# A second seven-product group in the output projection of a two-layer decoder trunk

## The chip, the core and the metric

The kernel runs on one core of one Trainium2 chip. The metric is the device time of one execution in microseconds (us), from a median of several runs. The engines that matter are TensorE (PE in the profile; PEld is its weight load, which runs beside the matmuls), VectorE (DVE), ScalarE (ACT), GpSimd (POOL, which here only issues DMAs, among them all that add to their destination) and SyncE (SP, which issues the plain loads).

## The reference, cut to what matters

Everything is float32: 256 tokens, 2048 features, 2 layers. In each layer one normalised input is multiplied by a wide matrix `w_in`, three branches (sparse attention, a convolution, stick-breaking attention) are computed from it, gated, projected, merged by sigmoid gates, and put through one output projection. A last norm closes the trunk.

```python
proj = h @ w_in                                   # h = rms_norm(x)
...
y_a = (dsa_attention(...) * silu(za)) @ w_a_out
y_b = (conformer_conv(...) * silu(zb)) @ w_b_out
y_c = (stick_breaking_attention(...) * silu(zc)) @ w_c_out
g = sigmoid(gates).reshape(b, s, N_BRANCH, D_MODEL)
merged = g[:, :, 0] * y_a + g[:, :, 1] * y_b + g[:, :, 2] * y_c
return x + merged @ w_out                         # w_out is 2048 x 2048
```

The change touches the last line, and the order of the work just ahead of it (the last gate columns and the last columns of `y_b`).

## The kernel before, in words

**Units and steps.** A weight matrix is read in units of 256 rows by 512 columns (512 KB, a tile `raw` of 128 x 1024). To keep float32 precision at the speed of the rounded type, each unit is split into two parts: ACT casts `wh` from it (`high`, line 255) and DVE subtracts to get `wl` (`low`, line 259). The activations are split the same way, once. A unit then takes three products: activation high by `wh`, low by `wh`, high by `wl`. A plain step (`plain`, line 431) does this for two token tiles and two 128-row blocks: 12 matmuls of 128x512, eight that need only `wh` and then four that need `wl`.

**Seven products.** `Seven` (line 459) works on the first half of the depth (1024 of 2048 rows) of two neighbouring blocks of 512 columns. Seen as a 2 by 2 block matrix it takes seven block products in place of eight. A product is named M1 to M7 and has two half-steps, a and b: one unit each, used for one token tile alone, so six matmuls. Seven products are 14 half-steps or 84 matmuls; four plain steps for each of two column blocks are 8 units and 96 matmuls. The group pays with sums of weight blocks. `homes` becomes the operand of M5, then of M6, then of M4; `third` that of M7. The sums are made by DVE (`first_sums`, `second_sum`) or by DMAs that POOL issues and that add into the tile (`first_adds` line 501, `last_sum` line 530). Four PSUM banks X, Y, Z, W hold the results; ACT copies X to Y after M1 and W to a buffer after M5, and DVE makes Z (after M6) and W (after M7) by a subtraction (`fork`, line 581). The activation sums that M5, M6, M7 and M3 need (`osums`) are made by `output_sums`.

**The order of the work.** Strings written by hand (`gather`) set the order of the steps: `g.M1a` is the first half of M1 of the group `g`, and a letter alone takes the next plain step of that list. `run` walks the list: the cast and the subtraction of a step are issued two steps (`PARTS`) ahead of its matmuls, its load five more (`LOADS`). Tiles `wh` and `wl` have three buffers each, `raw` has five with a sixth place called `va`. A scheduler then fixes the order on each engine; each engine runs its own list strictly in that order.

**Around the change.** In each layer the last gate group (`h1`, 14 half-steps, with the plain steps `e1` and `f1` of its two column blocks) runs beside the products of `y_b`, 16 plain steps `y1` in four column blocks j = 0 to 3. When a block j is done, DVE merges it (lines 1568, 1569), transposes it in two pieces (line 299), POOL writes it to DRAM (four `z`, line 302) and reads it back (`zy`, line 308), and ACT and DVE split it into the operand `mx` (lines 667, 668), which the output projection needs from depth j*512 on. Then comes the output projection, four column blocks of 512 in lists `qs`. Before the change one group `o` takes two of them for the first half of the depth (blocks 2 and 3 in layer 0, blocks 0 and 1 in the last layer); the other two, `c` and `d`, run in plain steps through all the depth. In the last layer the first half of block 3 is four plain steps into a wide tile, and its second half is a tail of its own that ends the program (lines 1776 on).

Of the kernel before, what the change touches and what calls it, by code (L numbers as in the profile page):

```python
# [51 lines left out]
def trunk(ctx: ExitStack, tc: tile.TileContext, x, w_in, xt, w_a, w_b, w_c, w_out,  # L52
# [63 lines left out]
    class Lazy(list):  # L116
        def __init__(self, n, make):
            super().__init__([None] * n)
            self.make = make
# [21 lines left out]
    def acc_tile():  # L141
        return ap.tile([P, 512], F32, tag="acc", bufs=4, name=nm("acc"))
# [316 lines left out]
    class Seven:  # L459


        def __init__(self, w, cols, act, sums, lead=7, own=None, adds=False, room=None):
            self.banks = banks = {}
            self.steps = {}

            def bank(n):
                if n not in banks:
                    banks[n] = acc_tile()
                return banks[n]
# [33 lines left out]
            def first_sums(h):  # L503
                if own is not None:
                    with in_turn():
                        raw = self.steps["M1", h].raw
                        nc.vector.tensor_add(raw, raw, homes[h])
                    return
                with in_turn():
                    if adds in (1, 2):  # L510
                        nc.vector.tensor_add(homes[h], homes[h], self.steps["M1", h].raw)
                        return
                    nc.vector.tensor_add(third[h], third[h], homes[h])
                    nc.vector.tensor_add(homes[h], homes[h], self.steps["M1", h].raw)

            def second_sum(h):
                if own is not None:
                    if adds:
                        nc.gpsimd.dma_start(homes[h], block(1, 1, h), accum_op=ALU.add)
                    with in_turn():  # L520
                        if not adds:
                            nc.vector.tensor_add(homes[h], homes[h], third[h])
                        nc.vector.tensor_add(third[h], third[h], self.steps["M1", h].raw)
                    return
                with in_turn():
                    nc.vector.tensor_add(homes[h], third[h], self.steps["M1", h].raw)

# [48 lines left out]

            st["M1", 1].at(0, partial(copied, "X", lambda: bank("Y")))
            st["M5", 1].at(0, partial(copied, "W", held))
# [190 lines left out]
    for layer in range(DEPTH):  # L769
# [864 lines left out]
        def merged(b, j, y):  # L1634
            sg = held.pop((b, j), None)
            with in_turn() if b == 1 else nullcontext():
                merge(b, j, y, sg)
            if b == 1:
                with in_turn():
                    turned([mg(j, t) for t in range(NT)], partial(use_m, j), LATER - 3 * (j == 3 and not last), soon=True)  # L1640

        kept_x, acc3 = {}, once(wide_accs)

        def output(q, banks, k0):
            if last and q == 3:
                return [plain(wo, k, q * 512, mx, acc3, k == 0, False) for k in range(0, KC, 2)]

# [66 lines left out]
        zg["M3", 1].at(1, partial(gate_summed, 1))  # L1714
        for i in range(2):
            y1[3][i].at(0, partial(output_sums, i * 2, i * 2 + 1))
        if last:
            zd[3].at(0, lambda: nc.sync.dma_start(fwl[0], fnw.partition_broadcast(P)))
        o = Seven(wo, (p0 * 512, p0 * 512 + 512), mx, osums, 10, None, 3)
        qs = {}  # L1720
        for q in range(4):
            own = q in (p0, p0 + 1)
            banks = (lambda v: lambda: [o.bank(n) for n in v])("ZW" if q - p0 else "XY") if own else None
            qs[q] = output(q, banks, KC if own else 0)
        begin = "g.M1a y g.M5a g.M1b y g.M5b y g.M6a y g.M6b y g.M2a y g.M2b y g.M7a y g.M7b "
# [13 lines left out]
        steps += gather(thin + rest, y=y2[10:], g=g1, c=c1, d=d1)  # L1739
        steps += gather("y*2 " + begin.replace("M6a y", "M6a").replace("M2a y", "M2a") + rest, g=h1, y=y1[:8], c=e1, d=f1)  # L1740
        steps += y1[8:]
        def no_products():
# [9 lines left out]
        steps[at_norm].at(0, norm)  # L1752
        c, d = 2 - p0, 3 - p0
        if last:
            steps += qs[c][:4] + gather(
                "g.M1a d g.M5a g.M1b d g.M5b d g.M6a d g.M6b c g.M2a c g.M2b g.M7a g.M7b g.M3a e g.M3b e g.M4a f g.M4b f c*2 e*2 f*2",
                g=o, c=qs[c][4:], d=qs[d], e=qs[p0], f=qs[p0 + 1])
        else:
            steps += qs[c][:4] + qs[d][:4] + gather(
                "g.M1a c g.M5a g.M1b c g.M5b d g.M6a d g.M6b c g.M2a c g.M2b d g.M7a d g.M7b g.M3a g.M3b e g.M4a e g.M4b e*2 f*4",  # L1760
                g=o, c=qs[c][4:], d=qs[d][4:], e=qs[p0], f=qs[p0 + 1])
        extra = []
# [12 lines left out]
        with tc.high_priority(offset=URGENT):  # L1775
            nc.vector.reduce_sum(known, ssq[:, :, :3], axis=AX.X)
            nc.vector.tensor_scalar(half, known, -0.5 / D, -0.5 * EPS, op0=ALU.mult, op1=ALU.add)
            nc.vector.tensor_scalar(known, known, 1.0 / D, EPS, op0=ALU.mult, op1=ALU.add)

        c0, n = 1536, 512  # L1780
        xc = residual(c0, n)

        head = acc3()
        accs = [head[0], acc_tile()]
# [100 lines left out]
```

## Time and profile before

| | |
|---|---|
| median of 3 runs | 1976.75 us (1975.53 to 1977.73) |
| the profiled execution | 1976.5 us |
| its span, first to last instruction | 1974.6 us |
| granted TensorE clock | 0.998 |
| busy: PE, DVE, ACT, POOL | 1964.4, 1714.8, 1350.3, 248.7 us |
| moved by DMA | 503.67 MB, mean 255 GB/s |

The profile describes one execution. A busy PE is not a PE at its peak, since matmuls overlap and their ends are modelled; the rate is read from the starts in the timeline. Idle time of an engine off the critical chain costs nothing by itself. Around the span lie 1.9 us that the trace does not show.

### The profile page before, as it was taken

The page shows a single profiled execution, that of the slowest core. Times are in us where ns is not written, and L with a number is a line of the kernel's source. Part 1 is how long each engine was busy: PE and PEld are TensorE (multiplying, and loading weights), DVE is VectorE, ACT ScalarE, POOL GpSimd, SP SyncE. Part 2 cuts the span into 40 slices and gives each one's busy share as a digit, 9 for nine tenths or more (in the row PEclk, how much of TensorE's full clock was granted, in tenths as well). Part 3 has the DMA queues.
Part 4 walks back from the last instruction along what each step waited for, and adds up shares of the span by engine and source line. Part 5 has one row for each costly group of instructions (what it writes and reads, how often), then busy time and mean ns, then how long its engine had stood idle before and what let it go on. Part 6 is the DMA issues. An engine that isn't in the chain of part 4 may idle for free.

```text
span 1974.6 us, 26301 instructions
## 1 busy us (share of the span) xinstructions
PE 1964.4 (99%) x9170; PEld 1644.9 (83%) x9170; DVE 1714.8 (87%) x2010; ACT 1350.3 (68%) x1774; POOL 248.7 (13%) x348
## 2 busy tenths in 40 slices
PE   9999999999999999999999999999999999999998
PEld 8888888888888888888888888888888888888886
DVE  8788999988898899878786988999889988898786
ACT  7567657679887667564565666676798876765654
POOL 0011102210200002111100211122101000011010
PEclk9999999999999999999999999999999999999999
DMA  8888769876888889887978887698769898899883
GB/s 277 278 256 271 236 188 313 265 226 190 251 271 262 237 246 298 265 269 274 319 229 277 250 268 234 200 291 279 221 178 283 255 286 245 249 294 270 272 292 136
DMA packets 256261, 503.67 MB, mean 255 GB/s; under 512 B 18496, under 2 KB 31296, under 8 KB 256000
## 3 DMA queue, kind: packets, MB, share of 16 engines
q1 hardware_dynamic: 218560, 408.13, 63.4%
q0 software_dynamic: 35904, 90.72, 18.2%
q10 hardware_dynamic: 1664, 3.15, 0.4%
q8 instruction: 71, 1.16, 0.2%
q14 instruction: 62, 0.51, 0.1%
HBM read 469.16 MB, written 32.77 MB: 254 GB/s over the span
## 4 chain that ended last, share of the span: by engine, by line
PE 99%; DVE 1%; ACT 0%; issue 0%; DVEq 0%
PE acc L270 67%; PE mm L270 28%; PE mm L1269 1%; PE mm L1360 0%; PE mm L1464 0%; PE mm L1411 0%; PE mm L1327 0%; PE mm L1441 0%; PE mm L918 0%; PE mm L1330 0%; PE mm L1240 0%; PE mm L1414 0%; PE mm L1469 0%; DVE wl L259 0%; DVE s L1831 0%; PE mm L1443 0%
## 5 line engine op out<-in xcount | busy, mean ns | idle before, releaser
L270 PE MATMUL acc<-wh,s 128*128 128x512 f32 x3952 | 1006.9, 390 | 0.0
L255 ACT CAST wh<-raw 128x1024 fp32r<-128x1024 f32 (+1 forms) x637 | 664.7, 1046 | 393.4 <-PE acc L270 240.9
L259 DVE TENSOR_TENSOR wl<-raw,wh 128x1024 fp32r<-128x1024 f32 (+1 forms) x638 | 770.0, 1213 | 167.2 <-ACT wh L255 162.8
L270 PEld LDWEIGHTS acc<-wh,s 128*128 128x128 f32 x3952 | 734.8, 188 | 148.2 <-ACT wh L255 0.6
L270 PE MATMUL acc<-wl,s 128*128 128x512 f32 x1784 | 498.9, 390 | 0.1
L270 PEld LDWEIGHTS acc<-wl,s 128*128 128x128 f32 x1784 | 333.8, 188 | 71.5 <-DVE wl L259 2.6
L270 PE MATMUL mm<-wh,s 128*128 128x512 f32 (+1 forms) x1504 | 366.5, 385 | 0.0
L270 PEld LDWEIGHTS mm<-wh,s 128*128 128x128 f32 x1504 | 281.2, 188 | 54.9
L302 POOL DMA_DIRECT2D z<-zt x192 | 114.6, 635 | 682.3 <-DVE zt L299 636.5
L270 PE MATMUL mm<-wl,s 128*128 128x512 f32 (+1 forms) x752 | 198.0, 385 | 0.0
L270 PEld LDWEIGHTS mm<-wl,s 128*128 128x128 f32 x752 | 140.7, 188 | 26.9
L255 ACT CAST wh<-ar 128x1024 fp32r<-128x1024 f32 x92 | 96.9, 1054 | 71.1 <-PE acc L270 32.5
L259 DVE TENSOR_TENSOR wl<-ar,wh 128x1024 fp32r<-128x1024 f32 x92 | 111.8, 1221 | 15.4 <-ACT wh L255 14.4
L259 DVE TENSOR_TENSOR wl<-va,wh 128x1024 fp32r<-128x1024 f32 x53 | 64.7, 1221 | 21.4 <-ACT wh L255 21.2
L255 ACT CAST wh<-va 128x1024 fp32r<-128x1024 f32 x53 | 55.5, 1046 | 32.7 <-PE acc L270 13.9
L308 POOL DMA_DIRECT2D zy<-z x50 | 37.0, 741 | 309.3 <-DVE s L668 86.8
L270 PEld LDWEIGHTS mm<-s,wl 128*128 128x128 f32 x512 | 66.9, 191 | 5.0
L733 DVE SCALAR_TENSOR_TENSOR s<-yT,cst,s 128x256 f32<-128x256 f32 x160 | 69.5, 478 | 0.0
L270 PE MATMUL mm<-s,wl 128*128 128x192 f32 x512 | 66.0, 271 | 0.0
L728 ACT ACTIVATE zt<-yT,cst 128x256 f32<-128x256 f32 x128 | 57.5, 502 | 8.2 <-DVE s L1037 8.0
L728 ACT ACTIVATE ar<-yT,cst 128x256 f32<-128x256 f32 x136 | 60.4, 503 | 2.9 <-PE mm L1330 2.3
L530 POOL DMA_DIRECT2D ar<-in_w_in_dram x28 | 33.8, 1217 | 187.1 <-DVE wl L259 152.0
(293 smaller groups left out, 1581.4 us busy)
## 6 DMA issues: line engine op xcount, KB each, us to landing
raw<-in_w_in_dram SPq DMA_DIRECT2D x496, 512.0 KB, 4.7
raw<-in_w_out_dram SPq DMA_DIRECT2D x50, 512.0 KB, 5.7
zy<-z POOLq DMA_DIRECT2D x48, 512.0 KB, 5.9
z<-zt POOLq DMA_DIRECT2D x184, 128.0 KB, 5.2
ar<-in_w_in_dram SPq DMA_DIRECT2D x28, 512.0 KB, 7.1
ar<-in_w_in_dram POOLq DMA_DIRECT2D x28, 512.0 KB, 8.4
raw<-in_w_a_dram SPq DMA_DIRECT2D x26, 512.0 KB, 6.0
raw<-in_w_b_dram SPq DMA_DIRECT2D x26, 512.0 KB, 5.1
```

The lines of the kernel that those rows point to most:

```text
L255: newest_parts[0] = nc.scalar.copy(u[1], u[0])
L259: newest_parts[1] = sub = nc.vector.tensor_sub(u[2], u[0], u[1].bitcast(F32))
L270: newest[0] = nc.tensor.matmul(o, lhsT, rhs, start=start, stop=stop, skip_group_check=True)
L302: nc.gpsimd.dma_start(z[:, :, :, a, :].rearrange("t b c e -> c (t b) e"), tmp[a * 32:(a + 1) * 32].rearrange("c t b k i -> c (t b) (k i)"))
L308: nc.gpsimd.dma_start(y.rearrange("p (t a) k i -> p t (a k i)", a=4), z.rearrange("t b c a e -> (b c) t (a e)"))
L530: nc.gpsimd.dma_start((homes if own is None else third)[h], block(1, 0, h), accum_op=ALU.add)
L728: nc.scalar.activation(v, yT[:, c, q:q + S], AF.Identity if bias else AF.Copy, scale=wq, **b)
L733: nc.vector.scalar_tensor_tensor(o, yT[:, c, q:q + S], wq, o, op0=ALU.mult, op1=ALU.add)
L1269: nc.tensor.matmul(ps[:, q * S:(q + 1) * S], qi[i][:, hd, :], ki[j][:, 0, :], start=n == 0, stop=n == 2)
```

## The change

A second group `n` is put on the two column blocks that had been plain, so that all four column blocks take the first half of the depth in seven products. Its first products stand earlier: M1 lies among the four plain steps `f1` of the last gate block (in the strings now `h`), M5 and M6 among the last four steps of `y1`, and M2 and M7 follow at once; then the two groups run into one another. The old group `o` gets PSUM from two wide tiles (`wide=True`) in place of four narrow ones, and two of the large slots (`places`) for its `homes` and `third`. Both groups take a new way with their sums (`adds` = 4): `homes` has M1's unit added once, the second sum is `third + homes` and no longer needs M1's raw unit, and what `third` lacked is added by a DMA that POOL issues after that. M1's copy from X to Y comes five steps later in `n` (`copy_at`). The turned block j = 1 is asked for three units sooner, and the activation sums are placed anew.

The diff, without the signature of `Seven` and the removal of the plain steps for the last block:

```diff
                 if n not in banks:
-                    banks[n] = acc_tile()
+                    if wide:
+                        banks.update(zip("XY" if n in "XY" else "ZW", wide_accs()))
+                    else:
+                        banks[n] = acc_tile()
...
-                    if adds in (1, 2):
+                    if adds in (1, 2, 4):
                         nc.vector.tensor_add(homes[h], homes[h], self.steps["M1", h].raw)
                         return
                     nc.vector.tensor_add(third[h], third[h], homes[h])
...
-                    nc.vector.tensor_add(homes[h], third[h], self.steps["M1", h].raw)
+                    nc.vector.tensor_add(homes[h], third[h], homes[h] if adds == 4 else self.steps["M1", h].raw)
+                if adds == 4:
+                    first_adds(h)
...
-            st["M1", 1].at(0, partial(copied, "X", lambda: bank("Y")))
+            st["M1", 1].at(copy_at, partial(copied, "X", lambda: bank("Y")))
...
-                    turned([mg(j, t) for t in range(NT)], partial(use_m, j), LATER - 3 * (j == 3 and not last), soon=True)
+                    turned([mg(j, t) for t in range(NT)], partial(use_m, j), LATER - 3 * (j in (1, 3)), soon=True)
...
-        for i in range(2):
-            y1[3][i].at(0, partial(output_sums, i * 2, i * 2 + 1))
+        for i, st in enumerate((y1[2][3], f1[0])):
+            st.at(0, partial(output_sums, i * 2, i * 2 + 1))
...
-        o = Seven(wo, (p0 * 512, p0 * 512 + 512), mx, osums, 10, None, 3)
...
+        c, d = 2 - p0, 3 - p0
+        places = [once(lambda: slot().rearrange("p a b -> p (a b)")) for _ in range(2)]
+        o = Seven(wo, (p0 * 512, p0 * 512 + 512), mx, osums, 10, None, 4, places, True)
+        n = Seven(wo, (c * 512, d * 512), mx, osums, 9, None, 4, None, False, 5)
...
+        second = "n.M1a h n.M1b h*3 y n.M5a y n.M5b y n.M6a n.M6b y n.M2a n.M2b n.M7a n.M7b "
         if last:
-            steps += qs[c][:4] + gather(
-                "g.M1a d g.M5a g.M1b d g.M5b d g.M6a d g.M6b c g.M2a c g.M2b g.M7a g.M7b g.M3a e g.M3b e g.M4a f g.M4b f c*2 e*2 f*2",
-                g=o, c=qs[c][4:], d=qs[d], e=qs[p0], f=qs[p0 + 1])
+            second += ("o.M1a c o.M1b c o.M5a o.M5b n.M3a n.M3b o.M6a o.M6b n.M4a n.M4b c o.M2a o.M2b o.M7a o.M7b c "
+                       "o.M3a e o.M3b e o.M4a f o.M4b f e*2 f*2")
         else:
...
+            second += ("o.M1a c o.M1b d o.M5a c o.M5b d o.M6a n.M4a o.M6b n.M4b c*2 o.M2a d o.M2b o.M7a o.M7b n.M3a n.M3b d "
+                       "o.M3a e o.M3b e o.M4a e o.M4b e f*4")
```

Counted over the whole program, 24 matmuls of 128x512 fall away (12 in each layer). There are 12 more units to split, in as many casts on ACT and subtractions on DVE, four more DVE sums of 128x1024 (eight for `n`, four fewer for `o`), and four more forks; ACT has four more copies between banks. DMAs of 512 KB: four more on SP, 12 more that add on POOL.

The first place is DVE in the last layer, where the last block of `y1` is merged and `o` begins. Before, in the list of DVE (`wl` are the subtractions of units, `t` and `s` with line 1569 the merge, `zt` the transposes, `ar`, `ph` and `pl` the sums of `o`; the first transposes are those of the block j = 3):

```order
L299 STREAM_TRANSPOSE zt_16533<-s_2546_13909 128x4x4x32 x2
L513 TENSOR_TENSOR ph_16353<-ph_16353,ar 128x1024
L259 TENSOR_TENSOR wl_16562<-raw_16449,wh_16561 128x1024
L514 TENSOR_TENSOR ar<-ar,raw_16449 128x1024
L259 TENSOR_TENSOR wl_16580<-raw_16476,wh_16579 128x1024
L259 TENSOR_TENSOR wl_16596<-ar,wh_16595 128x1024
L513 TENSOR_TENSOR pl_16410<-pl_16410,ar 128x1024
L526 TENSOR_TENSOR ar<-ph_16353,raw_16449 128x1024
L514 TENSOR_TENSOR ar<-ar,raw_16512 128x1024
L259 TENSOR_TENSOR wl_16612<-raw_16512,wh_16611 128x1024
```

And now, from the subtraction of n.M2b on (line 673 is the split of `mx` for j = 2, `ph` and `pl` are the operands of n.M7, `s_3083` is `homes` of `o`, line 586 the fork of W in `n`; the last two rows are o.M1a and the first step of `c`):

```order
L259 TENSOR_TENSOR wl_16608<-raw_16525,wh_16607 128x1024
L673 TENSOR_TENSOR s_3096_16623<-zy_16452,s_3096_16623 128x4x256
L259 TENSOR_TENSOR wl_16630<-ph_16263,wh_16629 128x1024
L1573 TENSOR_TENSOR t_3070_16507<-mm_16494,t_3070_16507 128x1024
L259 TENSOR_TENSOR wl_16651<-pl_16306,wh_16650 128x1024
L1574 TENSOR_TENSOR s_2559_13938<-s_2559_13938,t_3070_16507 128x1024
L514 TENSOR_TENSOR s_3083_16559<-s_3083_16559,raw_16578 128x1024
L299 STREAM_TRANSPOSE zt_16641<-s_2559_13938 128x4x4x32 x2
L586 TENSOR_TENSOR acc_16516<-ev_16557,acc_16523 128x512
L259 TENSOR_TENSOR wl_16662<-raw_16578,wh_16661 128x1024
L259 TENSOR_TENSOR wl_16674<-raw_16591,wh_16673 128x1024
```

The merge and the transposes of block 3 used to stand among plain steps of 12 matmuls; now they stand among half-steps of six.

The second place is PE at the same point. Before, the group begins with one half-step between plain ones (`mm` is the tile of `d`):

```order
L270 MATMUL acc_16599<-wh_16561,s_3001_16183 128x512 x4
L270 MATMUL acc_16599<-wl_16562,s_3001_16183 128x512 x2
L270 MATMUL mm_16615<-wh_16579,s_3001_16183 128x512 x8
L270 MATMUL mm_16615<-wl_16580,s_3001_16183 128x512 x4
L270 MATMUL acc_16632<-wh_16595,s_3053_16446 128x512 x4
L270 MATMUL acc_16632<-wl_16596,s_3053_16446 128x512 x2
```

Now (n.M7a and n.M7b, then o.M1a into the wide tile and the first step of `c`):

```order
L270 MATMUL acc_16523<-wh_16629,s_3046_16370 128x512 x4
L270 MATMUL acc_16523<-wl_16630,s_3046_16370 128x512 x2
L270 MATMUL acc_16523<-wh_16650,s_3046_16370 128x512 x4
L270 MATMUL acc_16523<-wl_16651,s_3046_16370 128x512 x2
L270 MATMUL mm_16691<-wh_16661,s_3014_16212 128x512 x4
L270 MATMUL acc_16381<-wh_16673,s_3096_16623 128x512 x4
L270 MATMUL acc_16523<-wh_16673,s_3096_16623 128x512 x4
L270 MATMUL mm_16691<-wl_16662,s_3014_16212 128x512 x2
L270 MATMUL mm_16691<-wh_16687,s_3014_16212 128x512 x4
```

The scheduler has put the eight matmuls of `c` that need only `wh` ahead of the two of o.M1a that need `wl`. In layer 0 the rows of both engines are the same up to here.

The third place is POOL in the last layer. Before (`z` and `zy` of j = 2, then of j = 3; `ar` are the adding DMAs of `o`):

```order
L302 DMA z_16432<-zt_16431 32x8x128 x4
L308 DMA zy_16494<-z_16432 128x2x512
L302 DMA z_16534<-zt_16533 32x8x128 x4
L530 DMA ar<-in_w_out_dram 128x2x512
L308 DMA zy_16675<-z_16534 128x2x512
```

Now (`ph`, `pl` and `ar` are adding DMAs of `n`, `s_3079` and `s_3083` those of `third` and `homes` of `o`):

```order
L302 DMA z_16391<-zt_16390 32x8x128 x4
L504 DMA ph_16263<-in_w_out_dram 128x2x512
L308 DMA zy_16452<-z_16391 128x2x512
L504 DMA pl_16306<-in_w_out_dram 128x2x512
L535 DMA ar<-in_w_out_dram 128x2x512 x2
L302 DMA z_16642<-zt_16641 32x8x128 x4
L308 DMA zy_16698<-z_16642 128x2x512
L504 DMA s_3079_16545<-in_w_out_dram 128x2x512 x2
L535 DMA s_3083_16559<-in_w_out_dram 128x2x512 x2
```

The read back of block 3 no longer stands behind an adding DMA, and eight adding DMAs stand where there were two.

More of the change, by code (lines that the diff above doesn't have):

```diff
@@ L459, in trunk, with __init__ @@
     class Seven:
-        def __init__(self, w, cols, act, sums, lead=7, own=None, adds=False, room=None):
+        def __init__(self, w, cols, act, sums, lead=7, own=None, adds=False, room=None, wide=False, copy_at=0):
             self.banks = banks = {}
@@ L1639, in merged @@
                 with in_turn():
-                    turned([mg(j, t) for t in range(NT)], partial(use_m, j), LATER - 3 * (j == 3 and not last), soon=True)
-        kept_x, acc3 = {}, once(wide_accs)
+                    turned([mg(j, t) for t in range(NT)], partial(use_m, j), LATER - 3 * (j in (1, 3)), soon=True)
+        kept_x = {}
         def output(q, banks, k0):
             if last and q == 3:
-                return [plain(wo, k, q * 512, mx, acc3, k == 0, False) for k in range(0, KC, 2)]
+                return []
             def finished():
@@ L1714, in trunk @@
         zg["M3", 1].at(1, partial(gate_summed, 1))
-        for i in range(2):
-            y1[3][i].at(0, partial(output_sums, i * 2, i * 2 + 1))
+        for i, st in enumerate((y1[2][3], f1[0])):
+            st.at(0, partial(output_sums, i * 2, i * 2 + 1))
         if last:
             zd[3].at(0, lambda: nc.sync.dma_start(fwl[0], fnw.partition_broadcast(P)))
-        o = Seven(wo, (p0 * 512, p0 * 512 + 512), mx, osums, 10, None, 3)
[L1720 to L1724, printed above, removed]
+        c, d = 2 - p0, 3 - p0
+        places = [once(lambda: slot().rearrange("p a b -> p (a b)")) for _ in range(2)]
+        o = Seven(wo, (p0 * 512, p0 * 512 + 512), mx, osums, 10, None, 4, places, True)
+        n = Seven(wo, (c * 512, d * 512), mx, osums, 9, None, 4, None, False, 5)
+        qs = {q: output(q, lambda g=g, v=v: [g.bank(i) for i in v], KC)
+              for q, g, v in ((c, n, "XY"), (d, n, "ZW"), (p0, o, "XY"), (p0 + 1, o, "ZW"))}
         begin = "g.M1a y g.M5a g.M1b y g.M5b y g.M6a y g.M6b y g.M2a y g.M2b y g.M7a y g.M7b "
@@ L1739, in trunk @@
         steps += gather(thin + rest, y=y2[10:], g=g1, c=c1, d=d1)
-        steps += gather("y*2 " + begin.replace("M6a y", "M6a").replace("M2a y", "M2a") + rest, g=h1, y=y1[:8], c=e1, d=f1)
-        steps += y1[8:]
+        steps += gather("y*2 " + begin.replace("M6a y", "M6a").replace("M2a y", "M2a") +
+                        "g.M3a c g.M3b c g.M4a c g.M4b c y*4", g=h1, y=y1[:12], c=e1)
         def no_products():
@@ L1752, in trunk @@
         steps[at_norm].at(0, norm)
-        c, d = 2 - p0, 3 - p0
+        second = "n.M1a h n.M1b h*3 y n.M5a y n.M5b y n.M6a n.M6b y n.M2a n.M2b n.M7a n.M7b "
         if last:
-            steps += qs[c][:4] + gather(
-                "g.M1a d g.M5a g.M1b d g.M5b d g.M6a d g.M6b c g.M2a c g.M2b g.M7a g.M7b g.M3a e g.M3b e g.M4a f g.M4b f c*2 e*2 f*2",
-                g=o, c=qs[c][4:], d=qs[d], e=qs[p0], f=qs[p0 + 1])
-        else:
-            steps += qs[c][:4] + qs[d][:4] + gather(
-                "g.M1a c g.M5a g.M1b c g.M5b d g.M6a d g.M6b c g.M2a c g.M2b d g.M7a d g.M7b g.M3a g.M3b e g.M4a e g.M4b e*2 f*4",
-                g=o, c=qs[c][4:], d=qs[d][4:], e=qs[p0], f=qs[p0 + 1])
+            second += ("o.M1a c o.M1b c o.M5a o.M5b n.M3a n.M3b o.M6a o.M6b n.M4a n.M4b c o.M2a o.M2b o.M7a o.M7b c "
+                       "o.M3a e o.M3b e o.M4a f o.M4b f e*2 f*2")
+        else:
+            second += ("o.M1a c o.M1b d o.M5a c o.M5b d o.M6a n.M4a o.M6b n.M4b c*2 o.M2a d o.M2b o.M7a o.M7b n.M3a n.M3b d "
+                       "o.M3a e o.M3b e o.M4a e o.M4b e f*4")
+        steps += gather(second, n=n, o=o, y=y1[12:], h=f1, c=qs[c], d=qs[d], e=qs[p0], f=qs[p0 + 1])
         extra = []
@@ L1778, in trunk @@
             nc.vector.tensor_scalar(known, known, 1.0 / D, EPS, op0=ALU.mult, op1=ALU.add)
+        head = [n.bank(i) for i in "ZW"]
         c0, n = 1536, 512
         xc = residual(c0, n)
-        head = acc3()
         accs = [head[0], acc_tile()]
```

## The prediction

> **What bounds the kernel now.** I read the page first: the busy times and the chain that ended last.
>
> ```profile
> PE 1964.4 (99%) x9170; PEld 1644.9 (83%) x9170; DVE 1714.8 (87%) x2010; ACT 1350.3 (68%) x1774; POOL 248.7 (13%) x348
> PE 99%; DVE 1%; ACT 0%; issue 0%; DVEq 0%
> ```
>
> The chain is TensorE alone. So a matmul less is time gained, as long as the engines that feed PE stay ahead. How little PE waits today is told by the waits, and its rate by the chain in order of time (143 matmuls of the last layer in one piece):
>
> ```profile
> PEld acc L270 <- DVE wl L259: 2.6, 10, 0.5
> ```
> ```profile
> 1859.96 32.41 PE mm L270 x143
> ```
>
> 32.41 / 143 = 0.2266 us for a matmul of 128x512; a plain step of 12 takes 2.72 us, a half-step of six 1.36 us. In the whole run PE lost 2.6 us to subtractions that came late. The question is whether VectorE can still keep up. The windows of the stage in layer 0 and in the last layer, and of its densest stretch:
>
> ```profile
> 880.00:1000.00 120.00, 120.00 (x531) 99.26 (x530) 97.67 (x109) 69.98 (x85) 20.02 (x31) 1.00 0.87 290
> 1860.00:1950.00 90.00, 90.00 (x398) 74.42 (x397) 74.89 (x77) 52.13 (x58) 8.53 (x12) 1.00 0.80 262
> 1887.00:1908.00 21.00, 21.00 (x94) 17.30 (x93) 20.06 (x19) 12.51 (x14) 4.33 (x7) 1.00 0.76 256
> ```
>
> The columns are PE, PEld, DVE, ACT and POOL busy, PE clock, DMA share, GB/s. PE is full and at full clock everywhere; DVE has 15.1 us free in 90, and is full for 21 us where group `o` begins. How far ahead DVE works is seen in the timeline, first among plain steps, then among half-steps: the cast of a unit, its subtraction, and the first matmul that uses it.
>
> ```profile
> 1877.90 1.05 ACT L255 CAST wh<-va 128x1024 fp32r<-128x1024 f32 x1 [1.67 <-PE mm L270]
> ...
> 1919.19 1.05 ACT L255 CAST wh<-raw 128x1024 fp32r<-128x1024 f32 x1 [0.76 <-PE acc L270]
> ```
> ```profile
> 1878.98 1.23 DVE L259 TENSOR_TENSOR wl<-va,wh 128x1024 fp32r<-128x1024 f32 x1 [1.03 <-ACT wh L255]
> ...
> 1920.28 2.59 DVE L259 TENSOR_TENSOR wl<-raw,wh 128x1024 fp32r<-128x1024 f32 x2 [0.59 <-ACT wh L255]
> ```
> ```profile
> 1885.86 1.07 PE L270 MATMUL mm<-wl,s 128*128 128x512 f32 x4
> ...
> 1923.07 0.61 PE L270 MATMUL acc<-wl,s 128*128 128x512 f32 x2
> ```
>
> With three buffers a cast starts when PE is through with the `wh` three steps back. Among plain steps the subtraction ends at 1880.2 and is needed at 1885.9: 5.7 us to spare. In a run of half-steps it ends at 1921.5 and is needed at 1923.1: 1.6 us to spare, room for one more DVE operation. And while PE takes 1.36 us for a half-step, DVE takes this:
>
> ```profile
> 1951.07 3.49 DVE L259 TENSOR_TENSOR s<-raw,s 128x1024 fp32r<-128x1024 f32 x3
> ```
> ```profile
> L668 DVE TENSOR_TENSOR s<-zy,s 128x1024 fp32r<-128x1024 f32 x3 | 3.7, 1218 | 0.0
> L299 DVE STREAM_TRANSPOSE zt<-s 128x512 f32<-128x512 f32 x4 | 2.6, 686 | 0.0
> L1569 DVE TENSOR_TENSOR s<-s,t 128x1024 f32<-128x1024 f32 x2 | 2.5, 1226 | 0.1
> L1568 DVE TENSOR_TENSOR t<-mm,t 128x1024 f32<-128x1024 f32 x2 | 2.4, 1217 | 0.0
> L514 DVE TENSOR_TENSOR ar<-ar,raw 128x1024 f32<-128x1024 f32 x2 | 2.4, 1217 | 0.0
> L581 DVE TENSOR_TENSOR acc<-ev,acc 128x512 f32<-128x512 f32 x2 | 1.4, 690 | 0.0
> ```
>
> An operation of 1024 lasts 1.22 us, but three in a row last 3.49, so the next starts after (3.49 - 1.22) / 2 = 1.135 us. A half-step with nothing beside it leaves DVE 1.36 - 1.135 = 0.22 us: it makes up almost nothing there.
>
> **The change part by part.**
>
> *Matmuls away.* 24 x 0.2266 = 5.44 us, all of it on the path. [...]
>
> *DVE, on average.* In the last layer: six more subtractions and two more sums, 8 x 1.22 = 9.8, two forks 1.4, together 11.2 us, while the stage loses 2.7 us. Of 15.1 free microseconds 1.2 are left (74.9 + 11.2 in 87.3 us, 99%). So where the work is uneven PE must wait. Layer 0 has the same additions in a stage with 22.3 us free.
>
> *DVE where it is densest.* Let T be the end of the last step of `y1`. Behind it PE has n.M2, n.M7 (four half-steps), o.M1a, and the first step of `c`. DVE cannot run ahead: the fork of Z must wait for n.M6b, which ends at T - 2.7; fork and the subtraction of M2b take it from T - 2.2 (M2a's subtraction comes first) to T - 0.4. Its list then has six operations of 1024 (split of `mx`, M7a, merge, M7b, merge, first sum of `o`), two transposes, a fork, and the subtraction of o.M1a: 6 x 1.135 + 1.2 + 0.6 + 1.2 = 9.8 us, so it ends at T + 9.4. PE gets there after 24 + 12 matmuls (the eight of `c` stand ahead): 36 x 0.2266 = 8.2 us. PE waits 1.2 us, in both layers, since both have these rows.
>
> *After that.* In the last layer eight half-steps follow in a row. From there to the subtraction of o.M6a DVE has 11 operations: nine that split a unit or make a first sum, and both second sums (11 x 1.135 = 12.5, T + 21.9). PE has 52 matmuls up to that point (11.8 us from T + 9.4: T + 21.2): 0.7 us more. From M6b on each step gives DVE its 0.22 us back, and with plain steps the wait ends. In layer 0 four steps of `d` stand in between, each with 2.72 - 1.135 = 1.6 us for DVE; nothing more is lost there. Sum of waits: 1.2 + 1.2 + 0.7 = 3.1 us, of which I give 1.5 to 6 as bounds: downward because a lag of DVE was swallowed today (21 us full and PE waited 0.16 us, the row below), upward by a DVE operation or two late in each layer.
>
> ```profile
> 1898.45 0.30 PEld L270 LDWEIGHTS acc<-wl,s 128*128 128x128 f32 x2 [0.16 <-DVE wl L259]
> ```
>
> [...]
>
> *ACT.* Twelve more casts and four copies. In the dense run it has one cast per half-step and two copies:
>
> ```profile
> L255 ACT CAST wh<-raw 128x1024 fp32r<-128x1024 f32 x25 | 26.4, 1055 | 24.8 <-PE mm L270 13.4 <-PE acc L270 8.5 <-DVE ph L513 1.7
> L667 ACT CAST s<-zy 128x1024 fp32r<-128x1024 f32 x3 | 3.1, 1042 | 0.0
> ```
>
> 1.06 of 1.36 us: it stays behind DVE in lateness and costs nothing; were DVE faster, it would be next.
>
> *The turn of block 3.* Step three of `c` needs `mx` of j = 3. The transposes end at about T + 7.6 by the list above; then four `z`, their landing, the read back:
>
> ```profile
> 1877.14 2.33 POOL L302 DMA_DIRECT2D z<-zt  x4 [31.42 <-DVE zt L299]
> 1885.37 0.72 POOL L308 DMA_DIRECT2D zy<-z  x1 [5.90 <-DMA z<-zt]
> ```
> ```profile
> zy<-z POOLq DMA_DIRECT2D x2, 512.0 KB, 7.9
> ar<-in_w_out_dram POOLq DMA_DIRECT2D x2, 512.0 KB, 10.7
> ```
>
> 8.2 us from the first `z` to the issue of `zy`, 7.9 to its landing, 1.04 for ACT: T + 24.7. PE comes there after 14 half-steps and two plain ones, 24.5 us, and with its 1.9 us of waiting at T + 26.4. Covered by 1.7 us. In layer 0 two more plain steps lie ahead. On POOL it is now ahead of the adding DMAs of `o`.
>
> *The adding DMA of `third`.* It waits on POOL for the second sum (T + 17.4 to 18.5), with only the last adding DMAs queued behind it. Landing takes 10.7 us: T + 28.1; with the cast T + 29.2. o.M7a stands at T + 30. Covered by 0.8 us; without cover it is paid whole.
>
> *Edits at nothing.* The wide tiles, the earlier turn of j = 1 and the new place of the activation sums fall mostly among plain steps with 5.7 us to spare. That a raw unit is let go earlier helps SP's queue, on which PE does not wait. The tail from the last step on has the same matmuls as before.
>
> Sum: 1976.5 - 5.4 + 3.1 = 1974.2 us on the profiled execution; this lies 0.25 us under the median, so 1974.4 us.
>
> **The rivals.**
>
> *The lag is swallowed.* If DVE enters T two operations ahead of my count, PE waits less than 1.5 us in all. For it: the swallowed 21 us above. Against it: the fork that ties DVE to n.M6b. 1971.3 to 1972.8, say 1972.0 us.
>
> *Covers that are too thin.* The read back of block 3 or the add into `third` lands 3 to 6 us later than the medians, beside more traffic. Only the last layer can lose by it: 1977.5 to 1980.5, say 1979 us.
>
> *DMA becomes the bound, and the kernel slower.* Each layer moves eight more units, 4.19 MB. The last layer's stage moved 262 GB/s x 90 us = 23.6 MB at a share of 0.80, so 3.05 us per MB: 12.8 us more. On average 72 + 12.8 of 87.3 us, 97%; but most of it falls into some 60 us, where at the stage's own share 48 are taken already, 54 at 0.90: 66.8 of 60 us, up to 6.8 us late. With layer 0 (0.87 x 60 + 12.8 = 65, 5 late) 11.8 us against 5.4: about 1983 us. It decides from 9.4 us of lateness on. Against it: loads are issued as buffers come free, some 5 units ahead, which hides unevenness. [...]
>
> *The change does not do what it says* is ruled out: the list of PE has 24 matmuls less.
>
> **How the numbers follow.** A measurement here can tell about 0.2% (3.95 us) from no change: faster means below 1972.8, slower above 1980.7. My forecast (waits of 1.5 to 6 us, 1972.8 to 1977.3) has 0.49; the swallowed lag 0.29; thin covers 0.10, which stay within 0.2%; DMA 0.12. So faster 0.29, same 0.59, slower 0.12. The range leaves out most of the DMA case and the lowest end of the swallowed lag: 1971.2 to 1981.0 us.
>
> **What would show it.** PEld waiting for `wl` at o.M1a about 1.2 us in each layer, and 0.7 us more before o.M6a in the last; DVE without idle from n.M2b to o.M6b; the rate of PE unchanged. If `wl` waits stay below 1.5 us in all, the second case holds. If ACT's casts wait for DMAs of `raw` or `third`, or DVE for `zy`, the third or the fourth. I am wrong at the root if the time moves while the matmul waits do not.

## The result, and the profile after

The changed kernel takes 1991.22 us (median of four runs, 1990.90 to 1993.64), the kernel before 1976.30 us in the runs beside it (1975.53 to 1977.73): a ratio of 1.0079, 95% interval 1.0064 to 1.0093. It is 15 us slower; 1974.4 us were forecast. The profiled execution took 1990.94 us, with a span of 1989.2 us.

The page of the changed kernel, busy times and chain:

```profile
PE 1965.8 (99%) x9146; PEld 1641.9 (83%) x9146; DVE 1736.0 (87%) x2033; ACT 1364.6 (69%) x1790; POOL 263.6 (13%) x360
PE 94%; DMA 3%; DVE 2%; ACT 0%; issue 0%; DVEq 0%; SPq 0%; ACTq 0%
```

The 24 matmuls are gone, and DVE has 21.2 us more to do. But the chain, which was 99% PE, now goes through DMAs for 3% of the span. The waits of the whole run name them: the first row is what PE's weight loads waited for, the next two what the casts of ACT waited for (in the kernel before no cast waited for a load of `w_out`).

```profile
PEld acc L270 <- ACT wh L255: 9.5, 5, 5.2
ACT wh L255 <- DMA raw<-in_w_out_dram: 10.0, 4, 4.5
ACT wh L255 <- DMA va<-in_w_out_dram: 9.0, 2, 5.9
```

The windows of the two stages, which were full for PE before:

```profile
880.00:1000.00 120.00, 114.70 (x492) 92.62 (x491) 103.93 (x110) 73.15 (x88) 27.28 (x37) 0.99 0.98 304
1860.00:1950.00 90.00, 81.50 (x343) 65.09 (x342) 77.41 (x81) 50.81 (x59) 15.85 (x18) 0.96 0.96 293
```

PE idles in both, and the DMA share has gone from 0.87 to 0.98 and from 0.80 to 0.96. Where PE loses its time is seen in its timeline of the last layer:

```profile
1869.82 1.98 PE L270 MATMUL acc<-wh,s 128*128 128x512 f32 x8
1872.53 1.20 PE L270 MATMUL acc<-wl,s 128*128 128x512 f32 x4 [0.74 <-DVE wl L259]
...
1881.74 0.61 PE L270 MATMUL acc<-wh,s 128*128 128x512 f32 x2
1883.47 0.73 PE L270 MATMUL acc<-wh,s 128*128 128x512 f32 x2 [1.12 <-DVE s L673]
...
1902.19 1.07 PE L270 MATMUL mm<-wh,s 128*128 128x512 f32 x4
1904.28 2.11 PE L270 MATMUL acc<-wh,s 128*128 128x512 f32 x8 [1.02 <-ACT wh L255]
...
1907.81 1.19 PE L270 MATMUL mm<-wh,s 128*128 128x512 f32 x4 [0.83 <-ACT wh L255]
1908.84 1.08 PE L270 MATMUL acc<-wl,s 128*128 128x512 f32 x4
1914.71 2.93 PE L270 MATMUL acc<-wh,s 128*128 128x512 f32 x6 [4.79 <-ACT wh L255]
1917.44 1.05 PE L270 MATMUL mm<-wl,s 128*128 128x512 f32 x2
1918.29 1.05 PE L270 MATMUL acc<-wh,s 128*128 128x512 f32 x2
```

To price a gap I take the distance from one row's start to the next one's and subtract 0.2266 us per matmul: 8 matmuls from 1869.82 take 1.81 us, the next row starts 2.71 later, so 0.90 us are lost. Done for every row of both stages, and each loss given to what the gap waited for (with the slower matmuls right behind it):

| lost by PE, us | layer 0 | last layer |
|---|---|---|
| subtraction of the third `h` step late (DVE) | 1.28 | 1.03 |
| low half of the activation sums late, in n.M5a (DVE) | 1.37 | 1.41 |
| fork of W late, ahead of the first step of `c` (DVE) | 1.51 | in the next row |
| units that landed late (first step of `c`, o.M1b, second step of `c`) | 4.59 | 10.03 |
| sum (0.12 elsewhere) | 8.75 | 12.59 |

21.3 us lost, 5.4 saved: 1974.6 + 15.9 = 1990.5 us, 1.3 above the span. Two thirds of the loss stand behind late loads. ACT and SP show how late (SP's rows: start, duration of the issue):

```profile
1906.71 1.05 ACT L255 CAST wh<-raw 128x1024 fp32r<-128x1024 f32 x1 [2.48 <-DMA raw<-in_w_out_dram]
1913.61 1.04 ACT L255 CAST wh<-va 128x1024 fp32r<-128x1024 f32 x1 [5.86 <-DMA va<-in_w_out_dram]
```
```profile
1882.84 5.11 SPq L425 DMA_DIRECT2D raw<-in_w_out_dram  x2
1888.00 8.09 SPq L1600 DMA_DIRECT2D t<-x  x3
1896.19 3.73 SPq L425 DMA_DIRECT2D va<-in_w_out_dram  x1
```

The load into `va` is `c`'s second unit. It stands behind three residual loads and is issued at 1896, and the issue alone took 3.73 us in place of 0.37. It landed 17.0 us later. The loads into `va`, in 1870:1960 of the kernel before and in 1885:1925 of the changed one:

```profile
DMA to landing us min/median/max: 3.6/5.6/7.8
```
```profile
DMA to landing us min/median/max: 8.1/12.5/17.0
```

The DMA view of the changed kernel, of 1920:1940 and of 1910:1920, says why everything is slow there (queue: packets, MB, share of the 16 engines' time; q0 is POOL's queue, q1 SP's):

```profile
q0 software_dynamic: 1063, 2.06, 58.3%
```
```profile
q1 hardware_dynamic: 1606, 3.09, 82.9%
```

In the first, q0 holds only the four adding DMAs of `o`: 11.66 us of all engines for 2.06 MB, 2.97 us for each 512 KB. In the second, the plain loads on q1 take 8.29 us for 3.09 MB, 1.41 us each. **By these two windows an adding DMA costs the DMA engines 2.1 times a plain load.** (The plain loads beside the adding ones in 1920:1940 took 36.7% for 2.34 MB, 3.1 us per MB; against those the ratio is 1.8.) The trace of before could have told: in its 1910:1920, q0 holds a plain read back and part of two adding DMAs.

```profile
q0 software_dynamic: 559, 1.31, 55.8%
q1 hardware_dynamic: 919, 1.78, 50.1%
```

5.58 us for 1.31 MB are 4.3 us per MB there, against 2.8 us on q1. I had charged bytes alone.

### The profile page after: what moved, and what is told of

Its sections match the earlier page's. It is cut to its first block, busy times and chain, and to the rows that moved or that the text cites. A ratio compares the mean times of both kernels' runs of the same rounds, so it can differ in the third digit from the quotient of the medians.

```text
span 1989.2 us, 26341 instructions
## 1 busy us (share of the span) xinstructions
PE 1965.8 (99%) x9146; PEld 1641.9 (83%) x9146; DVE 1736.0 (87%) x2033; ACT 1364.6 (69%) x1790; POOL 263.6 (13%) x360
## 4 chain that ended last, share of the span: by engine, by line
PE 94%; DMA 3%; DVE 2%; ACT 0%; issue 0%; DVEq 0%; SPq 0%; ACTq 0%
PE acc L270 64%; PE mm L270 27%; DMA va<-in_w_out_dram 2%; DMA ar<-in_w_out_dram 1%; DVE wl L259 1%; PE mm L1274 1%; PE mm L1365 0%; PE mm L1469 0%; PE mm L1332 0%; PE mm L1416 0%; DMA raw<-in_w_out_dram 0%; ACT wh L255 0%; PE mm L1446 0%; PE mm L923 0%; PE mm L1335 0%
## 5 line engine op out<-in xcount | busy, mean ns | idle before, releaser
L255 ACT CAST wh<-raw 128x1024 fp32r<-128x1024 f32 x635 | 662.0, 1046 | 370.1 <-PE acc L270 225.4
L270 PE MATMUL mm<-wh,s 128*128 128x512 f32 (+1 forms) x1520 | 373.8, 386 | 1.1 <-ACT wh L255 1.1
L270 PE MATMUL mm<-wl,s 128*128 128x512 f32 (+1 forms) x760 | 203.5, 387 | 0.0
L255 ACT CAST wh<-va 128x1024 fp32r<-128x1024 f32 x51 | 53.4, 1047 | 34.3 <-PE acc L270 11.5
```

The source lines that it names most:

```text
L255: newest_parts[0] = nc.scalar.copy(u[1], u[0])
L270: newest[0] = nc.tensor.matmul(o, lhsT, rhs, start=start, stop=stop, skip_group_check=True)
```

## The experiments

Theory A: the DMA engines are full in a stretch of some 40 us in each layer (in windows of 10 us the share is 1.01 to 1.10 in 1880:1920 and in 900:940), because adding DMAs cost the double (2.97 against 1.41 us), and units land late. Theory B: the residual loads stand in SP's list ahead of the units that PE needs. Theory C, later D: VectorE is late. Each run is compared with the kernel before on the same chip (medians 1975.6 to 1975.9 us). What "comes back" below is a difference of two medians; the kernel before differs by up to 0.7 us between these chips.

| label | median us (lowest to highest, runs) | ratio to before, 95% interval |
|---|---|---|
| e1_plain_adds | 1979.67 (1978.32 to 1981.56, 10) | 1.0019, 1.0009 to 1.0028 |
| e2_no_adds | 1979.32 (1977.74 to 1981.53, 10) | 1.0017, 1.0008 to 1.0027 |
| e3_x_behind | 1981.77 (1979.63 to 1983.69, 6) | 1.0029, 1.0017 to 1.0041 |
| e4_pool_sums | 1989.93 (1988.94 to 1991.07, 4) | 1.0070, 1.0053 to 1.0087 |
| e5_sums_later | 1979.89 (1976.11 to 1983.34, 11) | 1.0022, 1.0013 to 1.0031 |
| e6_sums_order | 1989.94 (1987.38 to 1991.00, 5) | 1.0070, 1.0057 to 1.0083 |
| e7_order_only | 1988.36 (1987.55 to 1990.89, 5) | 1.0068, 1.0054 to 1.0082 |
| e8_early_homes | 1982.23 (1978.20 to 1985.99, 7) | 1.0030, 1.0019 to 1.0041 |
| e9_early_no_swap | 1980.88 (1976.13 to 1983.75, 11) | 1.0022, 1.0014 to 1.0031 |
| e10_early_y_first | 1980.78 (1977.85 to 1983.62, 10) | 1.0025, 1.0015 to 1.0034 |
| e11_early_plain_adds | 1975.23 (1973.42 to 1978.19, 11) | 0.9998, 0.9989 to 1.0007 |
| e12_early_only | 1982.35 (1980.32 to 1985.77, 5) | 1.0036, 1.0022 to 1.0050 |

**The addition taken out, the DMA kept.**

```diff
-                nc.gpsimd.dma_start(third[h], block(0, 1, h), accum_op=ALU.add)
+                nc.gpsimd.dma_start(third[h], block(0, 1, h), accum_op=ALU.bypass if adds == 4 else ALU.add)
```

(and the same edit in `last_sum`)

> The eight adding DMAs of each layer's output projection (first_adds and last_sum of groups n and o) load the same blocks over the tile instead of adding them to it: the same bytes, the same queue, the same waits, only the addition is left out (so the output is not the reference's). In the trace of the changed kernel an adding DMA takes the 16 engines about 2.97 us (four of them 11.66 us in 1920:1940), a plain load of the same size about 1.41 us (3.09 MB in 8.29 us in 1910:1920). Theory A (the DMA engines are the bound in this stage because an adding DMA costs them twice a plain one): 8 x 1.56 = 12.5 us of DMA time less per layer, the casts hardly wait for loads any more, 1976 to 1981 us. Theory B (the residual loads that stand in a row ahead of the loads that PE needs): little changes, 1986 to 1991 us. Theory C (VectorE is late): nothing changes, 1989 to 1992 us.

11.5 us of the 15 come back, with the same bytes on the same queue: theory A's number, not B's or C's. PE waits for no load any more in either stage. In this run's 1880:1900 q0 holds only plain loads and a read back:

```profile
q0 software_dynamic: 743, 2.68, 34.8%
```

That is 6.96 us for 2.68 MB, 1.36 us for each 512 KB, where adding took 2.97. The edit changes one thing more: without the addition these packets are of 3.6 KB on average, with it of 1.9 KB (1063 for 2.06 MB). The size is not what costs, since SP's plain loads have packets of 1.9 KB too (1606 for 3.09 MB) and take 1.41 us.

What is left is VectorE, at the same places in both layers. PE's timeline of the last layer:

```profile
1868.55 1.21 PE L270 MATMUL acc<-wl,s 128*128 128x512 f32 x4 [0.60 <-DVE wl L259]
...
1879.48 0.72 PE L270 MATMUL acc<-wh,s 128*128 128x512 f32 x2 [1.08 <-DVE s L673]
...
1901.16 1.19 PE L270 MATMUL acc<-wh,s 128*128 128x512 f32 x4 [0.96 <-DVE acc L586]
```

**The adding DMAs taken out altogether.** The two `dma_start` stand behind `if adds != 4:`.

> The same eight adding DMAs of each layer are left out altogether (the output is not the reference's); everything else, VectorE's sums too, stays. Theory A: 8 x 2.97 = 23.8 us of DMA time less per layer; what remains are the waits for VectorE that the prediction counted, 1972 to 1977 us. If that holds, the gap between this run and the one with plain loads is what the bytes cost, and the gap from there to the changed kernel is what the addition costs. Theory B: residual loads still stand in a row, 1982 to 1990 us. Theory C: 1989 to 1992 us.

No further gain, and above the 1972 to 1977 us of theory A: with the addition gone the bytes are hidden, and VectorE costs more than the prediction counted. PE's losses in this profile sum to 10.1 us, all behind VectorE, and 1974.6 - 5.4 + 10.1 = 1979.3 us is the span measured. So without the adding DMAs the change, as it stands, would still be slower than before by some 3.5 us.

**The residual loads later.**

```diff
-                kept_x[q] = residual(q * 512, 512)
+                with issue_after(last_raw[0].ins):
+                    kept_x[q] = residual(q * 512, 512)
...
-            steps[-1].at(1, finished).at(-4, ask)
+            steps[-1].at(1, finished).at(-8, ask)
```

> All work is kept. The residual loads of the blocks are asked for eight steps ahead of a block's last step in place of four, but tied behind the last weight load asked for by then, so that they do not slip ahead of the weight loads in SP's list (three in a row stood ahead of the second unit of c in the last layer, two in layer 0). Theory A: as many bytes and adding DMAs; three loads of 1.41 us leave the densest stretch in the last layer and two in layer 0, 4 to 7 us of the loss come back, 1984 to 1988 us. Theory B: the loss goes nearly whole, 1974 to 1980 us. Theory C: nothing, 1989 to 1992 us.

9.5 us come back, more than A expected of so few bytes, less than B claimed. Late loads still cost 3.8 us in the last layer (a wait of 1.89 us at the first step of `c`, 1.7 us of slow matmuls behind it). Either edit by itself takes most of the loss away, so the two do not add up; that leaves open whether it is the loads' bytes or their place in the list. The run e12_early_only, below, tells that.

**The last sums on GpSimd.**

```diff
                 if adds > 1:
+                    if adds == 4:
+                        nc.gpsimd.tensor_add(homes[h], homes[h], self.steps["M2", h].raw)
+                        return
```

> All work is kept. The last sums of n and o (four of the eight adding DMAs of a layer) are made by GpSimd from the raw unit of M2, which is in SBUF anyway, in place of a DMA that adds. How long GpSimd takes for such a sum no row shows. Theory A: 4 x 2.97 = 11.9 us of DMA time less per layer, 1976 to 1983 us, if GpSimd is through before the cast of M4 needs the sum and does not slow VectorE. Theory B: 1985 to 1990 us. Theory C: 1989 to 1992 us, or more if VectorE's operations get longer beside GpSimd's.

Four adding DMAs less per layer, and nothing gained. The groups of 1870:1930 in this kernel:

```profile
L259 DVE TENSOR_TENSOR wl<-raw,wh 128x1024 fp32r<-128x1024 f32 x14 | 21.0, 1522 | 0.0
...
L259 DVE TENSOR_TENSOR wl<-ar,wh 128x1024 fp32r<-128x1024 f32 x6 | 10.6, 1772 | 0.7 <-ACT wh L255 0.6
...
L536 POOL TENSOR_TENSOR s<-s,raw 128x1024 f32<-128x1024 f32 x2 | 7.8, 3914 | 1.6 <-DVE wl L259 1.6
```

VectorE's subtraction takes 1.52 and 1.77 us on average where it took 1.21 and 1.22 in the changed kernel: 20 of them, 7.6 us. The long ones are those beside a GpSimd sum (2.94 us at 1889.32, 3.39 at 1893.35), the others still take 1.21: GpSimd's sums slowed VectorE down here. The waits for loads became waits for VectorE (up to 1.88 us for `wl`). This was the expectation's condition, not its number.

**VectorE's wait for the first homes.** In e3_x_behind DVE stood still ahead of the first sum of `n`, with all later work queued behind it:

```profile
1859.49 1.23 DVE L514 TENSOR_TENSOR ar<-ar,raw 128x1024 f32<-128x1024 f32 x1 [3.36 <-DMA ar<-in_w_out_dram]
```

The edit, on top of e3_x_behind (only `n` has `copy_at`):

```diff
-                st["M1", h].at(-PARTS + (own is not None), partial(first_sums, h), True)
+                st["M1", h].at((0 if copy_at else -PARTS) + (own is not None), partial(first_sums, h), True)
```

> The version with the residual loads tied behind weight loads (1981.8 us), and with group n's two first sums two steps later in VectorE's list. There, in the last layer, VectorE stood 3.36 us at 1856 waiting for n's homes to land, with all later work queued behind it, and was full from 1859 to 1886; PE then lost 1.14 us at the subtraction of the third h step and 1.41 us at the low half of the activation sums in n.M5a, and 0.91 and 1.37 us at the same two places of layer 0: 4.8 us together. Theory D (VectorE waits in order for the landing, and what it loses there comes out at these two places): the four losses go, about 1977 us (1976 to 1978.5). Theory A alone (only the DMA engines count): no change, 1981 to 1983 us. If VectorE just has too much to do there, with or without that wait, the losses shrink little: 1980 to 1982 us.

In the profile that wait of DVE is gone, and so are the two losses in the last layer (2.6 us). In layer 0 they stay, 0.53 and 1.28 us: there VectorE has simply too much to do. The median fell by 1.9 us, not 4.8, to just below the range of the third outcome. The profiled execution (1977.39 us) is one of the good ones, 2.5 us under the median, so its rows show less loss than the median has. Theory D is half right at most.

**Two steps exchanged.** On top of e5_sums_later:

```diff
-            second += ("o.M1a c o.M1b c o.M5a ...
+            second += ("o.M1a o.M1b c*2 o.M5a ...
```

(`...` stands for the rest of a line; likewise in layer 0)

> As the one before, and o.M1b stands right behind o.M1a, ahead of the first step of c, in both layers. The first step of c has to wait for the fork into bank W, which VectorE's lag makes late (0.96 us of waiting and 0.3 us of slow matmuls behind it in layer 0, 1.89 us beside a late load in the last layer). o.M1b gives the fork 1.36 us more. Theory D: 1.3 us in layer 0 and as much in the last layer come back, 1974 to 1976 us, about 2.5 us under the one before. Rival: the lag then ends at the subtraction of o.M1b or of the first c step, which are next in VectorE's list, and less than 1 us comes back: within 1 us of the one before.

10 us slower, against both expectations. The scheduler kept eight matmuls of `c` right behind the first four of o.M1a; they need `c`'s unit, which the exchange made the third to be loaded there in place of the second. PE's timeline of the last layer:

```profile
1901.88 1.07 PE L270 MATMUL mm<-wh,s 128*128 128x512 f32 x4
1907.30 3.78 PE L270 MATMUL acc<-wh,s 128*128 128x512 f32 x8 [4.35 <-ACT wh L255]
```

So it did not test the fork. It shows how little cover the loads have: asking for one unit earlier cost 10 us.

**The same two edits without moving the residual loads.**

> The changed kernel with the later first sums and o.M1b ahead of c, but with its own residual loads. In the changed kernel PE lost about 8 us to VectorE and 14 us to late loads with the slow matmuls behind them. If the two add up, 7 to 8 us come back: 1983 to 1985 us. If PE, sooner at the late loads, waits for them as much longer (the DMA engines have the same bytes to move in that stretch), little comes back: 1987 to 1991 us. I expect the second.

1988.36 us, in the range of the second. It has the wait at the first step of `c` of e6_sums_order, longer (5.59 us), so it says no more than that one.

**Four plain loads earlier.** On top of e6_sums_order the `lead` of `o` goes from 10 to 14.

```diff
-        o = Seven(wo, (p0 * 512, p0 * 512 + 512), mx, osums, 10, None, 4, places, True)
+        o = Seven(wo, (p0 * 512, p0 * 512 + 512), mx, osums, 14, None, 4, places, True)
```

> As e6_sums_order, with the four plain loads of group o's third and homes asked for four steps earlier. In the last layer they were issued at 1874 to 1878, just ahead of the stretch in which the DMA engines have a share of 1.0; in the 10 us before that stretch the share was 0.6 to 0.8. Theory A: 2.1 MB, 5.6 us of the 16 engines, leave the full stretch, and what PE still loses to late loads in the last layer (about 4 us in e3_x_behind) goes or halves: 2 to 4 us under e6_sums_order, 1971 to 1974 us. Rival: the adding DMAs fill the stretch by themselves, or the earlier loads only make n's own loads late: within 1 us of e6_sums_order, or slower.

7.7 us come back by one edit that only asks for 2.1 MB earlier. The size is above theory A's 2 to 4 us.

**The same early loads, the order as it was** (e5_sums_later with `lead` 14).

> The changed kernel with three edits: residual loads tied behind weight loads, n's first sums two steps later, group o's four plain loads four steps earlier; the order of the steps is its own again (o.M1a, c, o.M1b). In e6_sums_order the swap of two steps did not give the fork time: PE's list kept eight matmuls of c at the same place, now with the third load ahead of them in place of the second, and PE waited 4.35 us for it; the early loads then took 7.7 us off that. Theory A (how many loads must land by a given matmul of the half-steps decides): what the early loads take off also shows here, 1975 to 1978 us. Rival: e5_sums_later has little left to gain from the DMA side, only VectorE's waits remain, 1979 to 1981 us.

1980.88 us: the rival. Against e5_sums_later the median gains nothing; once the residual loads are gone from the stretch, the next 2.1 MB bring no more. In the profile the waits for casts in the last layer (1.15 and 0.88 us in e5_sums_later) are gone, but in layer 0 one of 1.60 us has come, behind the read back of block 3.

**One step of `y1` ahead of n.M5a.** On top of that one:

```diff
-        second = "n.M1a h n.M1b h*3 y n.M5a y n.M5b y n.M6a ...
+        second = "n.M1a h n.M1b h*3 y*2 n.M5a n.M5b y n.M6a ...
```

> As the one before, and in both layers the step of y1 that stood between n.M5a and n.M5b stands ahead of both, so that the low half of the activation sums, for which PE waited 1.0 to 1.1 us in n.M5a, is needed 2.7 us later. Theory D: about 1.2 us less in each layer where that wait is left (2.4 us if in both): 1973 to 1976 us. Rival: two half-steps in a row need their loads and subtractions sooner and the wait only moves to n.M5b: within 1 us of the one before.

The wait for the low half of the sums is gone in both layers, and the median has not moved: the rival. PE comes sooner to the next places and waits there: 0.7 to 0.8 us at n.M7b and 1.5 at the fork ahead of `c` (0.96 in e1_plain_adds) in both layers, and in layer 0 2.52 us for a cast that stands on ACT behind the split of `mx` for j = 3. ACT's row there:

```profile
937.95 1.04 ACT L672 CAST s<-zy 128x1024 fp32r<-128x1024 f32 x1 [4.79 <-DMA zy<-z]
```

The read back of block 3 is late, in a stretch of adding DMAs.

**The mended version without the addition.** The edit of e1_plain_adds on top of e10_early_y_first.

> As the one before, with the eight adding DMAs of each layer as plain loads over the tile (the addition is left out, so the output is not the reference's). If the adding DMAs still cost PE time in the mended version, it shows here: theory A 2 to 4 us less, 1970 to 1973 us, near the 1970.5 us that 24 matmuls less would give by themselves. Rival: what is left is VectorE's lag at the fork before the first step of c, which this does not touch: within 1 us of the one before.

5.6 us less than with the addition, and level with the kernel before. That is more than theory A's 2 to 4 us, though the 1970 to 1973 us are not reached; the rival is refuted. The pair shows the price directly. GB/s of the 16 engines in the 20 us from the issue of the first of `n`'s adding DMAs, in 40 slices: with the addition (1883.2:1903.2), then without it (1877.8:1897.8, since this run is ahead by 5.4 us there). From there on the same DMAs are asked for in the same order and at nearly the same distances:

```profile
GB/s 287 397 401 401 393 418 414 393 385 397 369 254 254 254 258 258 262 262 270 262 258 254 246 258 258 266 266 270 258 262 250 258 258 266 270 270 262 262 258 254
```
```profile
GB/s 397 401 389 385 397 393 401 381 410 369 389 369 385 389 369 389 397 393 385 402 381 393 369 373 385 393 381 385 393 393 307 172 86 45 25 4 0 0 0 0
```

With additions among them the engines move about 260 GB/s at a full share and are still at it at the end; without, they move about 390 and nearly all is done after 16 us. PE's losses in this profile are 2.4 and 2.2 us, mostly at the fork ahead of `c` (0.96 us of waiting in each layer).

**Early loads alone**, in the changed kernel: bytes or place.

> The changed kernel with one edit: the four plain loads of group o's third and homes are asked for four steps earlier; the residual loads stay where they are, three in a row ahead of c's second unit, and so does all else. 2.1 MB (5.6 us of the 16 engines) leave the stretch that is full from about 1880 on. Theory A (what counts is how many microseconds of DMA work lie in that stretch, whichever loads they are): a recovery of the order that moving the residual loads gave (9.5 us, by 1.57 to 2.1 MB in the last layer and 1.05 in layer 0): 1981 to 1986 us. Theory B (the residual loads' place in SP's list, ahead of the unit that PE needs, is the cause): no recovery, 1989 to 1992 us.

8.9 us come back, and all three residual loads (`t<-x`) still stand ahead of `c`'s second unit (`va`) in SP's list; one of them has slipped ahead of a weight load, so they are no longer three in a row:

```profile
1879.39 0.46 SPq L1600 DMA_DIRECT2D t<-x  x1
1883.71 0.37 SPq L425 DMA_DIRECT2D raw<-in_w_out_dram  x1
1884.13 3.12 SPq L1600 DMA_DIRECT2D t<-x  x2
1889.09 1.91 SPq L425 DMA_DIRECT2D va<-in_w_out_dram  x1
```

Theory B expected no recovery and is refuted: the amount of DMA work in the stretch is enough to account for it. PE waits for no load in layer 0 any more, but still 1.93 us for that unit in the last layer, so whether the place of the residual loads costs something besides is not shown.

No version that does the whole computation beats the kernel before. The mended ones scatter over 4 to 8 us from run to run (e5_sums_later 1976.1 to 1983.3), where the kernel before scatters over 2.1 to 2.6; what decides between a good and a bad run of them stays open.

## Why the prediction was wrong, point by point

- **Matmuls away, 5.44 us**: right. 24 less, and a plain step still takes 2.72 us.
- **DVE at o.M1a, 1.2 us in each layer**: right in mechanism and nearly in size. VectorE came about 1 us late, but at the fork one row ahead (0.96 us in e1_plain_adds, in both layers), since eight matmuls of `c` stand there. With the slower matmuls behind it the term is 1.3 to 1.5 us per layer.
- **0.7 us before o.M6a**: 0.17 us of waiting in e1_plain_adds. VectorE had caught up more.
- **Edits at nothing**: wrong. The earlier first sums and the activation sums among the `h` steps filled VectorE from 1862 to 1889 (26.3 of 27 us), and 5.7 us to spare were not enough: about 2.5 us in each layer, 5.1 together. I had counted VectorE's list from T on only.
- **The two covers** (read back of block 3, adding DMA of `third`): both held in the changed kernel, where PE waits for neither. It came there late, for other reasons, which helped them. In e9_early_no_swap and e10_early_y_first, with PE sooner, the first one fell in layer 0, where I had seen more room: 1.6 and 2.5 us of waiting.
- **The step that failed**: the sum (5.4 us saved, 3.1 us of waits for VectorE) carried nothing for the DMAs. Late loads, with the slower matmuls behind them, cost 14.6 of the 21.3 us that PE lost. The third rival had the mechanism and the side (1983 us, a chance of 0.12), but priced 4.19 MB at 3.05 us per MB, 12.8 us. It gave 5 us of lateness in layer 0 and 6.8 in the last; late loads cost 4.6 and 10.0 (the second with the last layer's fork in it). Six adding DMAs at 2.97 and two plain loads at 1.41 are 20.6 us of DMA time per layer: 72 + 20.6 = 92.6 in a last stage of 87.3 us, a share of 1.06. Full stretches read 1.01 to 1.10 here, so with the price per kind the average by itself says that nothing is left to cover unevenness. "Loads are issued some 5 units ahead, which hides unevenness" fell too: among half-steps a unit is needed each 1.36 us, 512 KB in that are 385 GB/s, and the engines gave about 260 to all queues together while additions ran (the slices of e10_early_y_first from the twelfth on).
- **The rate of the engines**: with additions in flight they moved those 260 GB/s, with none 391 (1910:1920 of the changed kernel). One price of 3.05 us per MB, as in the third rival, fits neither.

Without the DMA trouble the forecast would still have been 5 us too low (e2_no_adds, 1979.3 us), by the VectorE terms: 10.1 us of losses in place of 3.1.

## What to carry to other kernels

Price DMAs by kind, from the trace: time of the 16 engines for an adding DMA and for a plain one (2.97 and 1.41 us for 512 KB here), not bytes, and add them up over the densest 20 or 30 us in place of the stage. When a change takes matmuls out in exchange for sums, ask how many microseconds of every other engine one saved microsecond of PE costs: here 5.4 us of PE took 21 us of VectorE and 41 us of DMA time, and there was no room for either. VectorE stood 3.36 us ahead of the first sum of `n` in e3_x_behind, with all later work queued behind it, so count an engine's list from the first moved operation on, not from the place that looks densest.

## What the runs showed of the hardware

A wait of PE cost more than its gap here. Windows of the changed kernel, before and after the row at 1914.71 (the last three columns are PE clock, DMA share and GB/s):

```profile
1910.00:1914.70 4.70, 0.00 (x0) 0.00 (x0) 0.01 (x1) 1.09 (x2) 0.72 (x1) 0.82 1.04 394
1914.70:1919.70 5.00, 4.99 (x12) 3.94 (x13) 3.45 (x3) 2.75 (x4) 0.00 (x0) 0.50 1.04 388
```

After a gap of 4.79 us PE ran at a granted clock of 0.50 for about 5 us: two matmuls from 1917.44 take 0.85 us, 0.425 each, and 2.4 us are lost behind the gap. A shorter gap did the same. In e4_pool_sums a gap of 1.51 us was followed by matmuls of nearly full rate, one of 1.88 us by matmuls of 0.43 us:

```profile
1907.14 1.20 PE L270 MATMUL acc<-wh,s 128*128 128x512 f32 x4 [1.51 <-DVE acc L589]
...
1930.85 1.08 PE L270 MATMUL mm<-wl,s 128*128 128x512 f32 x2 [1.88 <-DVE wl L259]
```

In these stages of all profiles no gap up to 1.60 us (e9_early_no_swap) was followed by such a stretch, and every one from 1.88 us on was. Those waits cost about 1.7 to 2.9 us more, which made 4 us of the 21 lost.

The issue of the load into `va` on SP, 0.37 us in this stage of the kernel before, took 3.73 us at 1896 in the changed kernel, where the DMA share was 1.08; the next load in the list was issued at 1900.02. At 1915.94, with a share of 1.04, such an issue took 0.37 us again.
